# Moving weight sums, partial results and raw-weight tiles in a two-layer hybrid kernel

## The chip, the cores and the metric

The kernel runs on one core of one Trainium2 chip. TensorE (PE) multiplies matrices, VectorE (DVE) and ScalarE (ACT) do elementwise work, GpSimd (POOL) a few small operations and the transfers that add, and SyncE (SP) issues nearly all other transfers. Each engine works through its own queue in order and waits at its head. The metric is the device time of one execution in microseconds, as a median over runs.

## What is computed

Two layers on 512 tokens of width 1024, each with a mixing part and a gated feed-forward; all of it is float32.

```python
for layer in range(DEPTH):
    a = rmsnorm(h, ln_mix_pre[layer])
    mem_n = rmsnorm(mem, ln_mem[layer])
    if layer < N_A_LAYERS:
        ...
        main = chunked_spatial_gating(u, v, w_spatial[layer], b_spatial[layer],
                                      ln_v_g[layer], ln_v_b[layer])
    else:
        ...
        main = forgetting_attention(q, k_s, v_s, log_f_s)
    mixed = jnp.concatenate([main, memory_attention(q_mem, mem_n, w_mem_kv[layer])], axis=-1)
    h = h + rmsnorm(mixed @ w_out[layer], ln_mix_post[layer])
    f = rmsnorm(h, ln_ffn_pre[layer])
    f = (jax.nn.silu(f @ w_ffn_gate[layer]) * (f @ w_ffn_up[layer])) @ w_ffn_down[layer]
    h = h + rmsnorm(f, ln_ffn_post[layer])
```

The feed-forward is 2816 wide (22 blocks of 128). The change touches it most.

## The kernel before

**Numbers in two parts.** Every float32 operand is cut by `split` (L266) into a high part, which ScalarE rounds, and a low part, which VectorE subtracts; `mm3` (L208) multiplies by three matmuls (high by high, high by low, low by high). So each block of weights costs one ScalarE cast `whi` and one VectorE subtraction `wlo` before PE can use it.

**Feed-forward with seven products.** `feed_forward` (L1171) runs blocks 0 and 1 in the ordinary way at the boundary before it. The other 20 blocks are taken in pairs, m = 2, 4, ... 20, and each pair of gate weights and of up weights is one `Seven` (L1028): the 2 by 2 blocks of weights a11, a12, a21, a22 are multiplied by seven products in place of eight, in the order 1, 7, (3 of the set before), 6, 4, 2, 5. A product is 12 matmuls of 256 columns. Product 7 needs the sum s3 = a11 + a21, and a21 + a22 goes into the place of a21 (L1055, L1056); products 6 and 3 need a further addition each (L1059, L1061). Product 4 adds to the bank of product 7, after ScalarE has copied that out (L1083).

**Sums made by DMA.** For the gate weights of m = 6 to 20, and for the down weights, `sums_ahead` (L162) makes the two sums in DRAM: SP issues a copy from DRAM to DRAM (a gate sum is one of 512 KB), and POOL an accumulating transfer on top of it, which waits for the copy. `to_sum` is the list of those still to make; each call makes one, queued in SP behind the last load of weights. Before the change `sets` (L1249) calls it ahead of each gate set and each up set, so that 16 sums a layer are made while the gate and up sets run. For such a gate set the sums are loaded in place of one block, and the quarter a22 apart (L1041). The up weights are summed by VectorE.

**Down pass.** After each pair m = 2 + 2j up to j = 7, `Down` (L1102) holds u0, u1 and t, and `straight` (L1255) adds product 2 of the block before into two PSUM banks `kept`. Then a first pass over the eight blocks takes products 0, 3, 6, 5, a second takes 1 and 4 (`first_pass` L1309, loop L1332); `tap` (L1289) adds the ends to `ys`, the sums of the down projection, in which the products of blocks 0 and 1 already stand. Blocks 18 and 20 follow as gate and up sets without a Down; they and their four down blocks end in the tail.

**Space.** Raw weights go through four tiles of 4 KB per partition (`raw_tile` L134): two per set, so that a load waits until the set but one before it is done with its tiles. `act` is a ring of 36 tiles of 2 KB, `plain` one of 12. The residual stream `h` (16 KB per partition) is written to DRAM as `kept_h` (L1201) while the feed-forward runs; its space, `room` (L1222), holds u1 of the eight blocks (L1228) and is given back before sets 18 and 20, when h is loaded again (L1361).

**Order.** The program's order gives priorities. A planner takes them and its own costs and fixes the order on each engine's queue (SP's and POOL's among them) before the kernel runs; an instruction whose inputs it sees ready earlier can be drawn forward. `behind` (L253) pins the instructions made inside it behind a given one on the same engine.

**POOL's other work.** The reciprocal roots of the norms run there (`rsqrt` L280): one per 128 tokens in the tails, two in each boundary (L312), one in layer A for the layer norm. `boundary` (L938) joins a tail, the norm and the first four blocks of the next stage.

Of the kernel before, what the change touches and what calls it, by code (L numbers as in the profile page):

```python
# [1 line left out]

# [40 lines left out]
def hybrid(ctx: ExitStack, tc: tile.TileContext, i: dict, out: bass.AP):  # L43
# [93 lines left out]
    def loaded(src):  # L137

        raw = raw_tile()
        last_load[0] = nc.sync.dma_start(raw, src)  # L140
        return raw

    def prepared(src, shape, eng=None):
# [4 lines left out]
        last_load[0] = nc.sync.dma_start(dst, src)  # L148
# [11 lines left out]
    two_sums, to_sum = {}, []  # L160
# [22 lines left out]
    def moving_pair(src, aside=False):  # L183

        raw = wp.tile([P, 1024], F32, tag="raw", name=name("raw"), bufs=4)
        last_load[0] = nc.sync.dma_start(raw.rearrange("p (m c) -> p m c", m=4), src)
# [401 lines left out]
    def layer_a():  # L588
# [83 lines left out]
        with tc.tile_pool(name="sgu", bufs=1) as lp:  # L672
# [148 lines left out]

            gate_inputs(0)
# [205 lines left out]
    class Seven:  # L1028
# [5 lines left out]
        def __init__(self, xs, w, layer, m, tag, rows, room=None):  # L1034
            self.xs, self.tag, self.rows, self.room = xs, tag, rows, room
            self.parts = {}
            if (w, layer, m) in two_sums:
                both, raw = loaded(two_sums[w, layer, m]), loaded(i[w][layer, m])
# [4 lines left out]
            else:  # L1043
                raw, more = loaded(i[w][layer, m]), loaded(i[w][layer, m + 1])
# [4 lines left out]
        def form(self, n):  # L1049

            a11, a12, a21, a22 = self.a11, self.a12, self.a21, self.a22
            if n == 7:
                if not self.summed:
                    self.s3 = temp("s3")
                    V.tensor_add(self.s3, a11, a21)  # L1055
                    V.tensor_add(a21, a21, a22)  # L1056
                return self.s3
# [44 lines left out]
    class Down:  # L1102
# [33 lines left out]
        def weights(self, which):  # L1136

            four = lambda t: t.rearrange("p (m c) -> p m c", m=4)
# [4 lines left out]
            elif which == 1:  # L1143
                raw, t = four(raw_tile()), four(temp("t"))
# [4 lines left out]
            else:  # L1149
                raw = raw_tile()  # L1150
# [20 lines left out]
    def feed_forward(layer, phase, xp, meanwhile=None):  # L1171
# [28 lines left out]
        close()  # L1200
        kept_h = dp.tile([P, KT, T], F32, tag=name("rows"), name=name("rows"))  # L1201
# [10 lines left out]
        ys = [[None] * 2 for _ in range(TB)]  # L1212
        kept = [ps("tr", s="x") for _ in range(2)]
        for tb, dh in [(t, d) for d in (1, 0) for t in range(2)] + [(t, d) for t in (2, 3) for d in range(2)]:
# [3 lines left out]
            if tb > 1 or dh:  # L1218
                ys[tb][dh] = plain("y")
                A.activation(ys[tb][dh], o, AF.Copy, scale=1.0 - 2 * dh)  # L1220
# [66 lines left out]
        one, two = [act("ua", F32) for _ in range(2)], [act("ub", F32) for _ in range(2)]  # L1287

        def tap(n):  # L1289

            for t in range(2):
                x, y = o[n][t], ys[t]
                z = ys[2 + t]
                if n == 0:
                    A.copy(one[t], x)
                    V.tensor_add(y[0], x, y[0])
                elif n == 3:
                    V.tensor_add(one[t], x, one[t])
                elif n == 6:
                    V.tensor_add(two[t], x, one[t])  # L1300
                elif n == 5:
                    V.tensor_add(z[0], x, z[0])
# [6 lines left out]
        def first_pass(j, some):  # L1309
            if 0 in some:  # L1310
                downs[j].weights(1)
# [10 lines left out]
        for t in range(2):  # L1322
            ys[t][0] = plain("y")
            A.copy(ys[t][0], kept[t])
# [6 lines left out]
        late = [(z, t, d) for z, d, some in ((2, 0, two), (2, 1, two), (0, 1, one)) for t in range(2)]  # L1331
        for j, d in enumerate(downs):  # L1332
            d.weights(2)
# [4 lines left out]
            if j < len(late):  # L1338
                z, t, dh = late[j]
# [351 lines left out]
```

## Time and profile before

| | us |
|---|---|
| median of 3 runs | 1109.92 |
| lowest and highest | 1109.91, 1111.99 |
| the profiled execution | 1112.7 |
| its span, first to last instruction | 1111.0 |
| granted TensorE clock | 0.998 of full |

In the span, layer A with its boundary runs to about 200 us, the first feed-forward to about 503, layer B from there to about 790, and the second feed-forward with its tail to the end. In rows of the profile, `out<-in` names the tiles written and read, buffer numbers left out; `x` counts instructions; what stands after the last bar, or in square brackets, is the idle time of the engine just before, and what ended it. A tile has the name that it was given first where space is shared, so `room` stands for u1 of a Down, and `s`, `u` for rows of a set.

### The profile page before, as it was taken

Reading aid. Unit: us, or ns where it says so; the run is one execution under the profiler, and the core shown is the slowest. Engines: PE = TensorE matmul, PEld = TensorE weight load, DVE = VectorE, ACT = ScalarE, POOL = GpSimd, SP = SyncE. Lnnn points to the kernel's source line nnn. Section 1 sums busy time; section 2 is a strip of 40 time slices with the busy share of each in tenths; the row PEclk is TensorE's granted clock in tenths of the full one; section 3 lists DMA queues with packets and bytes.
Section 4 is the critical chain, followed back from the end, with each engine's and each line's share of the span. In section 5 each row is a group of like instructions: output and inputs, shape, how many; then the busy total and the mean of one; then the engine's idle time right before and its main releaser. Section 6 shows DMA issues by size and latency. Waiting matters only on the chain.

```text
span 1111.0 us, 19990 instructions
## 1 busy us (share of the span) xinstructions
PE 1086.8 (98%) x7286; PEld 984.2 (89%) x7286; DVE 936.6 (84%) x1839; ACT 729.6 (66%) x1609; POOL 59.6 (5%) x74
## 2 busy tenths in 40 slices
PE   9999999999999899999999999999999999899997
PEld 7998889999999888998988898889999999888996
DVE  7889658998877999996987798858898887999975
ACT  7776468666565667676765677768665665666563
POOL 0100001001100000000000000011011010000000
PEclk9999999999999999999999999999999999999999
DMA  7422346499888545653222654545489888544622
GB/s 267 157 81 76 96 114 199 115 239 220 217 204 203 144 130 152 218 171 127 84 92 75 173 127 108 148 114 171 125 220 235 219 210 217 143 124 135 215 77 76
DMA packets 126379, 172.69 MB, mean 155 GB/s; under 512 B 7821, under 2 KB 91801, under 8 KB 126281
## 3 DMA queue, kind: packets, MB, share of 16 engines
q1 hardware_dynamic: 114920, 153.93, 45.3%
q0 software_dynamic: 10944, 17.30, 10.3%
q8 instruction: 57, 0.93, 0.3%
q14 instruction: 42, 0.34, 0.1%
q10 hardware_dynamic: 416, 0.18, 0.1%
HBM read 155.04 MB, written 39.85 MB: 175 GB/s over the span
## 4 chain that ended last, share of the span: by engine, by line
PE 71%; DVE 12%; DMA 6%; ACT 6%; issue 4%; POOL 0%; SPq 0%; DVEq 0%; POOLq 0%; ACTq 0%
DVE wlo L268 5%; PE y L210 4%; PE y L211 4%; PE y L212 4%; DMA raw<-in_w_up 3%; PE a L210 3%; PE a L211 3%; PE a L212 3%; PE ps L212 3%; PE ps L211 3%; PE ps L210 3%; PE p L210 3%; PE p L212 3%; PE p L211 3%; ACT whi L267 2%
## 5 line engine op out<-in xcount | busy, mean ns | idle before, releaser
L267 ACT CAST whi<-raw 128x512 fp32r<-128x512 f32 x476 | 285.8, 619 | 93.9 <-DMA raw<-in_w_gate 24.4
L268 DVE TENSOR_TENSOR wlo<-raw,whi 128x512 fp32r<-128x512 f32 x476 | 318.3, 684 | 28.8 <-ACT whi L267 23.0
L210 PE MATMUL a<-xshi,whi 128*128 128x256 f32 x480 | 135.4, 282 | 2.0 <-ACT e L1094 2.0
L211 PE MATMUL a<-xslo,whi 128*128 128x256 f32 x480 | 134.7, 281 | 0.0
L212 PE MATMUL a<-xshi,wlo 128*128 128x256 f32 x480 | 134.5, 280 | 0.0
L210 PEld LDWEIGHTS a<-xshi,whi 128*128 128x128 f32 x480 | 90.3, 188 | 4.1 <-ACT e L1094 3.3
L211 PEld LDWEIGHTS a<-xslo,whi 128*128 128x128 f32 x480 | 90.4, 188 | 0.7
L212 PEld LDWEIGHTS a<-xshi,wlo 128*128 128x128 f32 x480 | 90.4, 188 | 0.0
L210 PE MATMUL e<-t,whi 128*128 128x256 f32 x160 | 47.2, 295 | 11.1 <-ACT s L1083 5.7
L211 PE MATMUL ps<-xslo,whi 128*128 128x256 f32 x192 | 53.9, 283 | 0.6 <-DVE xslo L268 0.6
L212 PE MATMUL ps<-xshi,wlo 128*128 128x256 f32 x192 | 54.3, 285 | 0.0
L210 PE MATMUL ps<-xshi,whi 128*128 128x256 f32 x192 | 53.6, 287 | 0.0
L210 PE MATMUL y<-whi,mixedhi 128*128 128x512 f32 x128 | 51.6, 403 | 0.0
L211 PE MATMUL y<-wlo,mixedhi 128*128 128x512 f32 x128 | 50.6, 395 | 0.0
L210 PE MATMUL p<-whi,ff 128*128 128x512 f32 x128 | 50.6, 396 | 0.0
L212 PE MATMUL y<-whi,mixedlo 128*128 128x512 f32 x128 | 50.4, 394 | 0.0
L211 PE MATMUL p<-wlo,ff 128*128 128x512 f32 x128 | 50.4, 394 | 0.0
L212 PE MATMUL p<-whi,ff 128*128 128x512 f32 x128 | 50.2, 394 | 0.0
L869 DVE TENSOR_TENSOR y<-y,y 128x512 f32<-128x512 f32 (+1 forms) x33 | 22.2, 673 | 30.4 <-PE y L212 30.3
L210 PE MATMUL e<-t3hi,whi 128*128 128x256 f32 x160 | 45.0, 281 | 0.0
L211 PE MATMUL e<-t,whi 128*128 128x256 f32 x160 | 45.0, 281 | 0.0
L210 PE MATMUL x<-xshi,whi 128*128 128x256 f32 x160 | 44.9, 281 | 0.0
(356 smaller groups left out, 3492.6 us busy)
## 6 DMA issues: line engine op xcount, KB each, us to landing
raw<-in_w_up SPq DMA_DIRECT2D x44, 512.0 KB, 4.5
raw<-in_w_gate SPq DMA_DIRECT2D x28, 512.0 KB, 4.6
raw<-in_w_down SPq DMA_DIRECT2D x28, 512.0 KB, 3.7
raw<-in_w_out SPq DMA_DIRECT2D x16, 512.0 KB, 4.5
sums<-in_w_gate SPq DMA_DIRECT2D x16, 512.0 KB, 6.0
sums<-in_w_gate POOLq DMA_DIRECT2D x16, 512.0 KB, 5.7
sums<-in_w_down SPq DMA_DIRECT2D x32, 256.0 KB, 4.8
sums<-in_w_down POOLq DMA_DIRECT2D x16, 512.0 KB, 6.9
```

The source lines that it names most:

```text
L210: PE.matmul(o, w[0], x[0], start=start, stop=False, skip_group_check=more)
L211: PE.matmul(o, w[0], x[1], start=False, stop=False, skip_group_check=more)
L212: return PE.matmul(o, w[1], x[0], start=False, stop=stop, skip_group_check=more)
L267: last_hi[0] = A.copy(hi, src)
L268: last_split[0] = last_hi[0], (eng or V).tensor_sub(lo, src, hi)
L869: (V.tensor_sub if turned_sign and dh else V.tensor_add)(y, o[:, cols], y)
```

## The change

It has four parts that share space.

1. `more_raws`: the space `room` becomes four raw tiles, handed out in turn. The up sets from m = 4 on (18 and 20 among them), the gate set m = 4, and every second block in both down passes take theirs there. So `room` is in use until the last up set, and h is loaded after that. u1 moves to the `plain` ring.
2. `kept_y`: the six results of the down products of blocks 0 and 1 that were kept in `plain` go to DRAM and are read back in the second pass, at j = 1 to 6. Four results of the taps now live in `act`, and the copies of `kept` in the two tiles tagged `acc`. The products of half 0 come first.
3. The eight gate sums of a layer are put on the list in layer A (for the first feed-forward) and in layer B (for the second). `load`, through which the loads of weights now go, counts 0.5 or 0.8 of a sum for each load and makes one whenever a whole one is due. In the feed-forward `sets` makes one down sum per pair, and none before the up set.
4. The two VectorE additions for an unsummed set are pinned behind the last split that was traced before them.

```diff
-    def loaded(src):
-        raw = raw_tile()
-        last_load[0] = nc.sync.dma_start(raw, src)
+    def loaded(src, raw=None):
+        raw = raw_tile() if raw is None else raw
+        load(raw, src)
         return raw
...
-    two_sums, to_sum = {}, []
+    two_sums, to_sum, credit = {}, [], [0, 0]
+
+    def load(dst, src):
+
+        last_load[0] = nc.sync.dma_start(dst, src)
+        credit[1] += credit[0]
+        if credit[1] >= 1:
+            credit[1] -= 1
+            sums_ahead()
...
+            to_sum.extend(("w_gate", 0, 6 + 2 * j) for j in range(8))
+            credit[0] = 0.5
             gate_inputs(0)
...
-                    V.tensor_add(self.s3, a11, a21)
-                    V.tensor_add(a21, a21, a22)
+                    with behind(last_split[0][1]):
+                        V.tensor_add(self.s3, a11, a21)
+                        V.tensor_add(a21, a21, a22)
...
-        for j in range(2, ones):
-            to_sum.append(("w_gate", layer, 2 + 2 * j))
-            if j > 2:
-                to_sum.append(("w_down", layer, 2 * j - 4))
-        to_sum.extend(("w_gate", layer, m) for m in (18, 20))
-        to_sum.extend(("w_down", layer, m) for m in (12, 14, 16))
+        to_sum.extend(("w_down", layer, 2 + 2 * j) for j in range(ones))
...
-        for tb, dh in [(t, d) for d in (1, 0) for t in range(2)] + [(t, d) for t in (2, 3) for d in range(2)]:
+        for tb, dh in [(t, d) for d in range(2) for t in range(2)] + [(t, d) for t in (2, 3) for d in range(2)]:
...
-                ys[tb][dh] = plain("y")
-                A.activation(ys[tb][dh], o, AF.Copy, scale=1.0 - 2 * dh)
+                y = plain("y")
+                A.activation(y, o, AF.Copy, scale=1.0 - 2 * dh)
+                nc.sync.dma_start(kept_y[tb, dh], y)
...
+        places_of_raws = cycle([room[:, 2 * n : 2 * n + 2, :].rearrange("p a b -> p (a b)") for n in range(4)])
+
+        def more_raws():
+            return next(places_of_raws)
...
-            downs.append(Down(layer, 2 + 2 * j, act("u", F32), room[:, j, :],
+            downs.append(Down(layer, 2 + 2 * j, act("u", F32), plain("u"),
...
             sums_ahead()
-            yield Seven(xs, "w_gate", layer, m, "mm", gate_rows)
-            sums_ahead()
-            yield Seven(xs, "w_up", layer, m, "lg", lambda row, u: up_rows(row, u, some), None if some else places)
+            yield Seven(xs, "w_gate", layer, m, "mm", gate_rows, raws=more_raws if m == 4 else None)
+            yield Seven(xs, "w_up", layer, m, "lg", lambda row, u: up_rows(row, u, some), None if some else places,
+                        more_raws if m > 2 else None)
...
                 if n == 0:
+                    one.append(act("ua", F32))
                     A.copy(one[t], x)
-                    V.tensor_add(y[0], x, y[0])
+                    y[0] = act("ya", F32)
+                    V.tensor_add(y[0], x, aside[t])
...
                 elif n == 5:
-                    V.tensor_add(z[0], x, z[0])
+                    z[0] = act("yb", F32)
+                    V.tensor_add(z[0], x, two[t])
...
-                downs[j].weights(1)
+                downs[j].weights(1, more_raws if j % 2 else None)
...
-            ys[t][0] = plain("y")
-            A.copy(ys[t][0], kept[t])
+            aside.append(temp("aside", tag="acc", bufs=2))
+            A.copy(aside[t], kept[t])
...
-            d.weights(2)
+            d.weights(2, more_raws if j % 2 else None)
...
-            if j < len(late):
-                z, t, dh = late[j]
-                y = ys[z + t][dh]
-                V.tensor_add(y, (two if z else one)[t], y)
+            if 0 < j < 7:
+                tb, dh, some = late[j - 1]
+                y = plain("y")
+                nc.sync.dma_start(y, kept_y[tb, dh])
+                if some is None:
+                    V.tensor_add(ys[tb][dh], y, ys[tb][dh])
+                else:
+                    V.tensor_add(y, y, some)
+                    ys[tb][dh] = y
...
+        to_sum.extend(("w_gate", 1, 6 + 2 * j) for j in range(8))
+        credit[0] = 0.8
         fill = queue([query_block(m) for m in range(2, 6)] + [value_block(0), key_block(0), key_block(1), value_block(1), key_block(2), key_block(3),
                       value_block(2), key_block(4), key_block(5)])
```

`prepared` and `moving_pair` load through `load` as well. After the boundary of a feed-forward `credit[0]` is set to 0 and the rest of the list is made at once; in layer B it is set to 0 when the output projection is laid out.

More of the change, by code (lines that the diff above doesn't have):

```diff
@@ L1043, in __init__ @@
             else:
-                raw, more = loaded(i[w][layer, m]), loaded(i[w][layer, m + 1])
+                raw, more = loaded(i[w][layer, m], raws()), loaded(i[w][layer, m + 1], raws())
                 self.a21, self.a22 = more[:, :512], more[:, 512:]
@@ L1286, in feed_forward @@
         o = {0: [ps("mm", s="p") for _ in range(2)], 3: [ps("lg", s="p") for _ in range(2)]}
-        one, two = [act("ua", F32) for _ in range(2)], [act("ub", F32) for _ in range(2)]
+        one, two, aside = [], [], []
         def tap(n):
@@ L1330, in feed_forward @@
         o.update({1: [ps("mm", s="q") for _ in range(2)], 4: [ps("lg", s="q") for _ in range(2)]})
-        late = [(z, t, d) for z, d, some in ((2, 0, two), (2, 1, two), (0, 1, one)) for t in range(2)]
+        late = [(2 + t, 0, None) for t in range(2)] + [(z + t, 1, some[t]) for z, some in ((2, two), (0, one))
+                                                       for t in range(2)]
         for j, d in enumerate(downs):
-            d.weights(2)
+            d.weights(2, more_raws if j % 2 else None)
             for n in (1, 4):
```

23 lines of the change are left out of this document (16 added, 7 removed).

## The prediction

> **What bounds the kernel now.** I read the page first: its busy line and its row of DMA tenths.
>
> ```profile
> PE 1086.8 (98%) x7286; PEld 984.2 (89%) x7286; DVE 936.6 (84%) x1839; ACT 729.6 (66%) x1609; POOL 59.6 (5%) x74
> DMA  7422346499888545653222654545489888544622
> ```
>
> TensorE is busy for 98% of the span, so nothing is to be won except where it waits, and the DMA row has two plateaus of 8 and 9 tenths. They are the gate and up stages of the two feed-forwards. The second view is the busy time by stage, with these two stages, what follows each, and stretches for comparison.
>
> ```profile
> 210.00:372.00 162.00, 156.81 (x1272) 153.23 (x1272) 136.86 (x240) 98.98 (x223) 13.92 (x13) 1.00 0.81 209
> 372.00:400.00 28.00, 26.00 (x141) 21.76 (x140) 27.15 (x52) 18.34 (x41) 0.00 (x0) 1.00 0.53 150
> 400.00:420.00 20.00, 20.00 (x88) 16.16 (x87) 19.21 (x37) 13.70 (x30) 0.00 (x0) 1.00 0.42 117
> 460.00:500.00 40.00, 40.00 (x336) 39.67 (x335) 37.42 (x66) 29.21 (x63) 1.14 (x2) 1.00 0.51 151
> 800.00:955.00 155.00, 151.08 (x1229) 147.80 (x1229) 131.80 (x230) 95.45 (x215) 14.01 (x13) 1.00 0.84 218
> 955.00:980.00 25.00, 23.03 (x136) 19.65 (x135) 24.15 (x47) 15.26 (x36) 0.00 (x0) 1.00 0.50 137
> 1040.00:1060.00 20.00, 20.00 (x171) 20.00 (x171) 18.98 (x32) 14.29 (x31) 0.00 (x0) 1.00 0.48 147
> ```
>
> Columns: the stretch, its length, busy time and instructions of PE, PEld, DVE, ACT and POOL, the granted clock, the DMA share, GB/s. The clock is full everywhere. The stretch 460 to 500 runs the same code on blocks 18 and 20 (gate sums ready in DRAM, no straight products and no new sums). There PE takes 40.00/336 = 0.119 us for a 256-column matmul, with DVE at 37.42 of 40. The stages of 162 and 155 us are slower per matmul at a DMA share of 0.81 and 0.84. Next I looked for what PE waits for in them: the groups of PE by line (205 to 400, then 795 to 985), and the list of waits (the same two stretches).
>
> ```profile
> L210 PE MATMUL e<-t,whi 128*128 128x256 f32 x64 | 19.1, 299 | 6.2 <-ACT s L1083 3.6 <-ACT room L1083 2.3
> L210 PE MATMUL e<-t,whi 128*128 128x256 f32 x64 | 19.0, 297 | 4.9 <-ACT room L1083 2.8 <-ACT s L1083 2.1
> ```
>
> ```profile
> ACT ff L267 <- DVE room L1239: 14.1, 6, 2.7
> DVE s L1055 <- DMA raw<-in_w_up: 13.9, 5, 3.2
> ...
> DVE s L1055 <- DMA raw<-in_w_up: 11.9, 6, 3.4
> ```
>
> Nearly all of PE's idle time is at one place, product 4 of a set, which cannot begin before ScalarE has copied product 7 out of the same bank (L1083). The timeline of one such case shows why that copy is late.
>
> ```profile
> 347.21 5.01 SPq L140 DMA_DIRECT2D raw<-in_w_up  x2
> ...
> 357.87 0.69 DVE L1055 TENSOR_TENSOR s<-raw,raw 128x512 f32<-128x512 f32 x1 [3.23 <-DMA raw<-in_w_up]
> ...
> 361.49 0.68 DVE L1239 SCALAR_TENSOR_TENSOR room<-room,s 128x512 f32<-128x512 f32 x1
> ...
> 362.26 0.41 ACT L267 CAST ff<-room 128x256 fp32r<-128x256 f32 x1 [2.71 <-DVE room L1239]
> 362.57 0.61 ACT L267 CAST whi<-raw 128x512 fp32r<-128x512 f32 x1
> 363.09 0.37 ACT L1083 COPY s<-e 128x256 f32<-128x256 f32 x1
> ...
> 363.51 0.19 PEld L210 LDWEIGHTS e<-t,whi 128*128 128x128 f32 x1 [1.47 <-ACT s L1083]
> ```
>
> The second load of the up block goes out at 347.21 + 5.01 - 0.33 = 351.9, since its tile is free only then; it lands near 357.8. VectorE has the sum s at the head of its queue and stands for 3.23 us with splits behind it. So room (L1239) is late, ScalarE waits 2.71 for it with the copy two places behind, and PE stands. One late load moves through DVE, ACT and PE.
>
> **The change part by part.** *Raw tiles and sums moved.* The up sets from m = 4 on, and the gate set m = 4, take their two tiles from the space of h, so that loads of either kind are two sets ahead instead of one. The eight gate sums of a layer, each one copy and one accumulate of 512 KB, leave the stage.
>
> ```profile
> raw<-in_w_up SPq DMA_DIRECT2D x44, 512.0 KB, 4.5
> ...
> sums<-in_w_gate SPq DMA_DIRECT2D x16, 512.0 KB, 6.0
> sums<-in_w_gate POOLq DMA_DIRECT2D x16, 512.0 KB, 5.7
> ...
> h<-rows SPq DMA_DIRECT2D x8, 512.0 KB, 9.9
> ```
>
> A set of seven products is 84 matmuls, 10 us, so a load that now starts two sets (20 us) ahead of its use has 14 us to spare over the 5.9 us that the bad one took. The up load's wait at DVE, 13.9 and 11.9 us, should go whole. What that is worth is PE's time: the matmuls of a stage at the rate of 460 to 500. The stage holds straight products, six matmuls of 512 columns each; by the groups of PE by shape there are three rows like this one, 36 in all, in either stage:
>
> ```profile
> L211 PE MATMUL x<-wlo,ff 128*128 128x512 f32 x12 | 4.7, 393 | 0.0
> ```
>
> They cost 20.00/88 = 0.227 us each by the row of 400 to 420. First layer: (1272 - 36) x 0.119 + 36 x 0.227 = 155.3, so 162.0 - 155.3 = 6.7 us. Second: 1193 x 0.119 + 8.2 = 150.2, so 155.0 - 150.2 = 4.8. Together **11.5**. Bounds: at the best rate seen, 20.00/171 = 0.117 from 1040 to 1060, it is 9.2 + 7.2 = 16.4; if no more than the half of the waits goes, 5.7. DVE is not in the way as long as it stays below PE: 136.86 us of work in the 155.3 us left is 88%, less than the 94% of the stretch I measure by.
>
> The Trainium skill (Perfetto Trace Analysis, Identifying the Most-Contended Engine) says that the busy share of matmuls is a poor measure of how near TensorE is to its limit, and that of weight loads a better one. By it the two stages, at 94.6% and 95.4% of weight loads against 99.2% in 460 to 500, would give 7.5 + 6.0 = 13.5 us, near the sum above; the page's 89% over the whole span would promise ten times that, and there the trace disagrees with the rule: 400 to 420 has 16.16 of 20 at PE's full pace, because a 512-column matmul hides its load.
>
> *The transition to the down pass*, 372 to 400 and 955 to 980: PE idles 2.0 us in each, with DVE at 27.15 of 28. The change gives DVE no less work, so I take 0; DVE might come in with less backlog, so at best 4.0.
>
> *Sums pinned.* The two additions of an up set are queued behind the split of that set's product 1, which reads the same tile. Without the pin, loads that come early would draw them further forward. No instruction is added; 0, with the waits above already counted.
>
> *First down products in DRAM.* Six tiles of 256 KB per layer are written behind ScalarE's copies and read back in the second pass, 12 transfers a layer. ScalarE's copies are the same six, DVE's additions the same count (the late ones run at j = 1 to 6 instead of 0 to 5, two taps take another operand). The writes stand in SP's queue for the copies; the loads behind them are those of m = 4, which so far went out 7 us after the last copy's end:
>
> ```profile
> 204.32 0.60 ACT L1220 ACTIVATE y<-y 128x512 f32<-128x512 f32 x1 [0.79 <-PE y L212]
> ...
> 212.20 0.94 SPq L140 DMA_DIRECT2D raw<-in_w_gate  x2
> ```
>
> DMA is at 0.42 in the down pass. I take 0; a read that is late stops DVE's addition and the splits behind it, at most one landing, 4.5 us by the row of the up loads, per layer.
>
> *h comes back later.* Its space is in use to the last up set. The last split of raw weights of the second feed-forward and the first residual addition:
>
> ```profile
> 1070.95 0.69 DVE L268 TENSOR_TENSOR wlo<-raw,whi 128x512 fp32r<-128x512 f32 x1 [0.16 <-ACT whi L267]
> ...
> 1088.84 0.86 DVE L907 SCALAR_TENSOR_TENSOR h<-yt,gains,h 128x128 f32<-128x128 f32 x3
> ```
>
> 17.2 us lie between, and the reload's landing took 9.9; 7 us to spare, cost 0. Were the cover gone, each us late would lengthen the end by one.
>
> *Four results now sit in the ring of 36* that also holds the memory inputs of the next layer.
>
> ```profile
> L272 ACT ACTIVATE mparts<-mem,gains x8: 493/502/511, 441.6 to 452.3; 128x256 fp32r<-128x256 f32 x8
> ...
> L210 PE MATMUL ps<-mparts,whi x16: 277/280/283, 490.4 to 497.3; 128*128 128x256 f32 x16
> ```
>
> They are made 38 us ahead of their use. With four places fewer, half of them or the first ff tiles wait for the last set to give up its inputs; eight casts of 0.5 us then fall at its end. 0, at worst 2.
>
> *Sums in layers A and B.* Sixteen copies in SP's queue behind loads, sixteen accumulates in POOL's. Stretches of those layers have room, and PE never waits there:
>
> ```profile
> 40.00:140.00 100.00, 99.92 (x606) 88.32 (x606) 82.75 (x185) 66.04 (x142) 1.64 (x2) 1.00 0.29 90
> 500.00:600.00 100.00, 100.00 (x640) 90.02 (x639) 82.09 (x188) 67.93 (x155) 7.10 (x12) 1.00 0.30 93
> ```
>
> But POOL also does the reciprocal roots on which the boundaries hang, in order, and an accumulate waits there for its copy. Before, this mixture was already there:
>
> ```profile
> 150.62 1.04 POOL L181 DMA_DIRECT2D sums<-in_w_gate  x1 [0.92 <-DMA sums<-in_w_gate]
> 154.61 0.57 POOL L281 TENSOR_TENSOR r<-v,mhalf 128x1 f32<-128x1 f32 x1 [2.95 <-DVE v L876]
> ...
> 183.53 0.88 POOL L181 DMA_DIRECT2D sums<-in_w_gate  x1 [1.21 <-DMA sums<-in_w_gate]
> 187.46 1.09 POOL L281 TENSOR_TENSOR r<-var,mhalf 128x2 f32<-128x2 f32 x1 [3.05 <-DVE var L311]
> ```
>
> Both times POOL was free again 3 us before the root's input came. I take **1.0** for one accumulate that stands in front of a root on the path; from 0 to 6.0 + 0.9 = 6.9 for each one that waits a whole landing.
>
> Sum: 11.5 - 1.0 = 10.5 us. The profiled execution ran 1112.7 (its span 1111.0 and 1.7 around it) and would come to 1102.2; the runs' median, 1109.92, lies 2.8 below it, so I expect **1099.4**.
>
> **The rivals.** *All stalls of both feed-forwards go*: best rate and no idle transitions, 16.4 + 4.0 = 20.4, 1089.5. For it: nothing but these stages stalls. Against: DVE at 27.15 of 28 in the transition.
>
> *Half only.* DVE and ACT keep an order in which product 4 waits for L1083 even when loads are early, or SP's queue is held by another transfer (the quarter a22 and the straight block share four small tiles), so loads don't start two sets ahead. For it: both layers idle 2.0 us in the transition, where no load is waited for. Against: the largest waits hang on the load. Half of 11.5 less 1.0: 1105.2. If the loads went out no earlier at all, the change would not do what it says: about 1110, within 0.2%.
>
> *Slower: POOL's queue.* Sums made near a boundary put accumulates in front of its roots, each waiting for a copy that stands behind a load in SP's queue. Price 6.9 us each on the path; it decides from the second one on (2 x 6.9 > 11.5), and with three, 20.7 - 11.5 = 9.2 us slower, 1119.1. For it: the tail's and boundary's own loads carry sums. Against: SP runs ahead there, so that the copies are done before most roots (the boundary's first gate load goes out 24 us before the root of 154.61), and the two cases above cost nothing.
>
> ```profile
> 130.82 0.34 SPq L148 DMA_DIRECT2D raw<-in_w_gate  x1
> ```
>  The Trainium skill (SBUF — State Buffer, the box on the "DVE blocks DMA" trap) adds that a DMA issued from POOL may stand while VectorE holds a port they share. The landings of 5.7 from POOL and 6.0 from SP for the same 512 KB, in stages where DVE is busy 85% of the time, show none of it.
>
> **How the numbers follow.** Forecast 0.60, all stalls gone 0.08, half only 0.13, no effect 0.04, slower 0.15. Faster by over 0.2% (2.2 us, about what a measurement of this kernel can tell from no change) is 0.60 + 0.08 + 0.13 = 0.81, less 0.02 for half cases eaten by the other costs: 0.79; same 0.04; slower 0.17. The forecast's own range is 1093.5 (16.4 gained) to 1105. The range reaches from 1091, short of the first rival, to 1112, which takes in the half and no effect and leaves out most of the slower case, some 0.18 in all.
>
> **What would show it.** Right: the waits of L1055 for raw<-in_w_up are gone, PE's idle time at product 4 falls from 6.2 and 4.9 us to below 2, the DMA share of the stages falls from 0.81 towards 0.5, and the stages are 6.7 and 4.8 us shorter. Layers A and B keep their length. Wrong: idle time at L1083 without a load behind it (half only), POOL's waits for sums ahead of L281 and ACT's for r L281 grown (slower), or DVE waiting for the reads of kept_y or h.

## The result and the profile after

The changed kernel took 1095.44 us, median of 4 runs (1094.50 to 1095.71), where the kernel before, measured beside it, took 1110.95 (4 runs, 1109.91 to 1112.79). The ratio is 0.9857, 95% interval 0.9840 to 0.9874: 15.5 us less. Measured a second time it took 1094.68 (1094.34 to 1095.10), ratio 0.9835 (0.9811 to 0.9860). The profiled execution, 1094.5 with a span of 1092.8, is 18.2 us shorter than the profiled one of before; the medians differ by less, because the profiled run of before lay 1.8 above its median and that of after 0.9 below.

The row of DMA tenths on the page of after:

```profile
DMA  7554875867644447267592654535877553546232
```

The plateaus of 8 and 9 in the feed-forwards are gone. Busy time of after by the stretches of the prediction (columns as there):

```profile
210.00:372.00 162.00, 161.99 (x1329) 159.81 (x1328) 148.59 (x252) 109.44 (x237) 6.22 (x5) 1.00 0.61 169
372.00:400.00 28.00, 28.00 (x123) 22.52 (x122) 27.43 (x55) 19.27 (x43) 0.00 (x0) 1.00 0.50 139
800.00:955.00 155.00, 155.00 (x1251) 151.87 (x1251) 142.71 (x248) 104.79 (x228) 6.25 (x5) 1.00 0.60 167
955.00:980.00 25.00, 25.00 (x109) 19.98 (x108) 24.43 (x48) 17.02 (x38) 0.00 (x0) 1.00 0.50 138
```

PE lacks 0.01 us in these 370, the transitions among them, where it had lacked 2.0 in each. The groups of PE by line, product 4 in 205 to 400 and in 795 to 985:

```profile
L219 PE MATMUL e<-t,whi 128*128 128x256 f32 x64 | 18.0, 281 | 0.0
...
L219 PE MATMUL e<-t,whi 128*128 128x256 f32 x58 | 16.3, 281 | 0.0
```

Idle time ahead of product 4 went from 6.2 and 4.9 to 0.0. VectorE's list of waits holds no wait for an up load any more.

To see where the 18.2 us are, four events serve as marks: the last copy of a first down product (ScalarE), the first root of layer B (GpSimd), that copy in the second feed-forward, and the first root of the tail. From the timeline of before (its first mark, 204.32, stands in the prediction):

```profile
511.32 0.57 POOL L281 TENSOR_TENSOR r<-v,mhalf 128x1 f32<-128x1 f32 x1 [9.85 <-DVE v L876]
...
790.89 0.60 ACT L1220 ACTIVATE y<-y 128x512 f32<-128x512 f32 x1 [0.79 <-PE y L212]
...
1085.66 0.57 POOL L281 TENSOR_TENSOR r<-v,mhalf 128x1 f32<-128x1 f32 x1 [150.34 <-DVE v L876]
```

and of after:

```profile
203.48 0.60 ACT L1233 ACTIVATE y<-y 128x512 f32<-128x512 f32 x1 [0.79 <-PE y L221]
...
500.01 0.57 POOL L290 TENSOR_TENSOR r<-v,mhalf 128x1 f32<-128x1 f32 x1 [9.39 <-DVE v L887]
...
781.45 0.60 ACT L1233 ACTIVATE y<-y 128x512 f32<-128x512 f32 x1 [0.79 <-PE y L221]
...
1067.91 0.57 POOL L290 TENSOR_TENSOR r<-v,mhalf 128x1 f32<-128x1 f32 x1 [185.97 <-DVE v L887]
```

The differences of neighbouring marks: first feed-forward 307.00 before, 296.53 after (10.47 less); layer B 279.57 and 281.44 (1.87 more); second feed-forward 294.77 and 286.46 (8.31 less). With 0.84 ahead of the first mark and 0.45 behind the last that makes the 18.2. So the feed-forwards gave 18.8 and layer B took 1.9 back. In the second measurement layer B took 280.34, 0.8 more than before, so that part of the loss differs from one execution to the next.

### The profile page after: what moved, and what is told of

Its sections match the earlier page's. It is cut to its first block, busy times and chain, and to the rows that moved or that the text cites. A ratio compares the mean times of both kernels' runs of the same rounds, so it can differ in the third digit from the quotient of the medians.

```text
span 1092.8 us, 20047 instructions
## 1 busy us (share of the span) xinstructions
PE 1080.9 (99%) x7286; PEld 982.6 (90%) x7286; DVE 941.6 (86%) x1839; ACT 736.9 (67%) x1609; POOL 59.4 (5%) x74
## 4 chain that ended last, share of the span: by engine, by line
PE 89%; ACT 3%; DMA 3%; DVE 2%; issue 1%; POOL 1%; SPq 0%; POOLq 0%; DVEq 0%; ACTq 0%
PE a L219 7%; PE a L221 7%; PE a L220 7%; PE e L219 3%; PE e L220 3%; PE e L221 3%; PE ps L221 3%; PE ps L220 3%; PE ps L219 3%; PE y L219 3%; PE y L220 3%; PE y L221 3%; PE p L219 3%; PE p L221 3%; PE p L220 3%; PE x L219 3%
## 5 line engine op out<-in xcount | busy, mean ns | idle before, releaser
L277 DVE TENSOR_TENSOR wlo<-raw,whi 128x512 fp32r<-128x512 f32 x316 | 210.8, 685 | 21.4 <-ACT whi L276 18.2
L276 ACT CAST whi<-raw 128x512 fp32r<-128x512 f32 x316 | 189.0, 619 | 56.2 <-PE a L220 14.6
L276 ACT CAST whi<-room 128x512 fp32r<-128x512 f32 x160 | 98.3, 621 | 47.9 <-PE x L220 9.5
L277 DVE TENSOR_TENSOR wlo<-room,whi 128x512 fp32r<-128x512 f32 x160 | 108.7, 686 | 6.4 <-ACT whi L276 3.8
L276 ACT CAST ff<-u 128x256 fp32r<-128x256 f32 x80 | 32.3, 406 | 29.3 <-PE p L221 15.4
L220 PE MATMUL x<-xslo,whi 128*128 128x256 f32 x160 | 44.9, 281 | 0.0
```

Source lines behind the costliest of these rows:

```text
L220: PE.matmul(o, w[0], x[1], start=False, stop=False, skip_group_check=more)
L276: last_hi[0] = A.copy(hi, src)
L277: last_split[0] = last_hi[0], (eng or V).tensor_sub(lo, src, hi)
```

## The experiments

Twelve runs. The columns F1, B and F2 are the three stretches above, in us, each from that run's one profiled execution. Where a feed-forward is the same as in after, F1 or F2 agrees with it within 0.06 us; B is less steady. Each ratio is to before measured beside the run; there the medians of before were 1111.29 (7 runs; the first four rows below after), 1112.43 (17; b_sums_moved_copies, a_again, a_sums_after_boundary, a_sums_in_boundary) and 1112.40 (23; the rest). One of the four executions of a_sums_in_ffn took 1106.08, which pulls its ratio up, and one of the ten of a_sums_in_boundary 2726, which nothing here explains.

| run | what it is | median us | ratio, 95% interval | F1 | B | F2 |
|---|---|---|---|---|---|---|
| (before) | | 1110.95 | | 307.00 | 279.57 | 294.77 |
| (after) | | 1095.44 | 0.9857 (0.9840 to 0.9874) | 296.53 | 281.44 | 286.46 |
| b_sums_moved | before + sums moved | 1098.01 | 0.9874 (0.9855 to 0.9893) | 297.36 | 280.48 | 288.23 |
| a_no_extra_raws | after, four raw tiles | 1097.60 | 0.9876 (0.9858 to 0.9894) | 297.54 | 282.35 | 287.19 |
| a_sums_in_ffn | after, sums as before | 1096.70 | 0.9895 (0.9847 to 0.9943) | 298.22 | 279.90 | 288.39 |
| a_no_pin | after, no pin | 1096.61 | 0.9867 (0.9847 to 0.9886) | 297.37 | 280.13 | 286.97 |
| b_sums_moved_copies | b_sums_moved + copies nothing reads | 1097.89 | 0.9862 (0.9835 to 0.9888) | 298.88 | 280.29 | 288.67 |
| b_pin | before + pin | 1097.82 | 0.9868 (0.9844 to 0.9893) | 298.61 | 279.91 | 289.05 |
| b_sums_moved_up_slot | b_sums_moved, sums ahead of the up set | 1109.96 | 0.9982 (0.9967 to 0.9996) | 303.51 | 280.54 | 294.88 |
| b_both_at_gate | before, both sums ahead of the gate set | 1112.86 | 0.9990 (0.9972 to 1.0008) | 309.12 | 280.43 | 293.11 |
| a_again | after | 1094.68 | 0.9835 (0.9811 to 0.9860) | 296.55 | 280.34 | 286.45 |
| a_sums_after_boundary | layer B's sums behind close() | 1095.08 | 0.9848 (0.9822 to 0.9874) | 296.58 | 286.50 | 286.45 |
| a_sums_in_boundary | layer B's sums in its boundary | 1108.73 | 0.9963 (0.9946 to 0.9980) | 305.37 | 285.53 | 286.46 |
| a_behind_roots | accumulates behind roots | 1101.97 | 0.9904 (0.9882 to 0.9926) | 296.59 | 288.74 | 286.44 |

### Which part carries the gain

**b_sums_moved**: before with the sums made as in the change (gate sums in layers A and B, down sums one for each pair of sets); four raw tiles, no pin.

```diff
-        for j in range(2, ones):
-            to_sum.append(("w_gate", layer, 2 + 2 * j))
...
+        to_sum.extend(("w_down", layer, 2 + 2 * j) for j in range(ones))
...
             yield Seven(xs, "w_gate", layer, m, "mm", gate_rows)
-            sums_ahead()
             yield Seven(xs, "w_up", layer, m, "lg", lambda row, u: up_rows(row, u, some), None if some else places)
```

> The kernel before, with only the gate sums moved into layers A and B; raw tiles, results in DRAM and order of the additions as before. Late loads (my theory: a load is late because it starts one set ahead AND lands slowly): the up load still starts when its tile is free, but lands in 4 to 4.5 us instead of 5.9, so that VectorE's wait for raw<-in_w_up falls from 13.9 and 11.9 us (two feed-forwards) to 4 to 7 each and PE's idle time at product 4 from 6.2 and 4.9 us to about 3 each: 1103 to 1106 us. Traffic alone (rival): the whole gain, 1095 to 1098 us, waits near 0. Buffers alone (rival): no gain, 1109 to 1111 us, waits above 11 us in each.

Measured 1098.01: my forecast missed, and this part alone gives nearly the whole gain. The waits for up loads did not go; they got shorter. The row of the waits of b_sums_moved (waiting line, releaser, sum, times, longest):

```profile
DVE s L1065 <- DMA raw<-in_w_up: 10.9, 10, 1.5
```

Those of before were up to 3.4, 25.9 us in 11. PE lacks 0.60 us in 205 to 400 here, where it lacked 7.19 before: the short waits hardly reach it, the long ones did.

**a_no_extra_raws**: after with the ring of four raw tiles everywhere.

```diff
-            return next(places_of_raws)
+            return raw_tile()
```

> The changed kernel with all raw weights in the four old tiles again; the space of h stands empty, everything else as changed. Late loads: as with the sums moved alone, 1102 to 1106 us, VectorE's waits for the up loads 3 to 7 us in each feed-forward. Traffic alone: 1095 to 1097 us. Buffers alone: 1109 to 1111 us.

1097.60, missed too. The tiles in the space of h are not needed for most of the gain.

**a_sums_in_ffn**: after with the sums asked for where they were before.

```diff
-            to_sum.extend(("w_gate", 0, 6 + 2 * j) for j in range(8))
-            credit[0] = 0.5
...
             yield Seven(xs, "w_gate", layer, m, "mm", gate_rows, raws=more_raws if m == 4 else None)
+            sums_ahead()
             yield Seven(xs, "w_up", layer, m, "lg", lambda row, u: up_rows(row, u, some), None if some else places,
                         more_raws if m > 2 else None)
```

> The changed kernel with the gate sums made in the feed-forwards again, two sums per pair; the extra raw tiles stay. Late loads: a load that starts two sets ahead has more than 10 us to spare even at a DMA share of 0.85, so 1095 to 1099 us with PE idle under 1.5 us at product 4 in each feed-forward. Traffic alone: 1107 us or more, with waits for up loads of over 8 us. Sums come too late for their sets (a third way): VectorE or ScalarE waits for raw<-sums, 1100 us or more.

1096.70, as forecast. The busy time of 210 to 372 of this run:

```profile
210.00:372.00 162.00, 160.63 (x1317) 158.25 (x1315) 147.21 (x250) 108.47 (x236) 13.01 (x12) 1.00 0.81 214
```

The DMA share is that of before, 0.81, but PE lacks 1.37 us of the 162 and not 5.19. A high share by itself costs little; in b_pin below PE lacks 0.70 at a share of 0.83.

**a_no_pin**: after with the two additions left free.

```diff
-                    with behind(last_split[0][1]):
-                        V.tensor_add(self.s3, a11, a21)
-                        V.tensor_add(a21, a21, a22)
+                    V.tensor_add(self.s3, a11, a21)
+                    V.tensor_add(a21, a21, a22)
```

> The changed kernel without the pin of the two additions of an up set. Late loads: the pin is worth little once loads are early, 1095 to 1098 us; additions are drawn forward but their data are there. The pin carries the gain (rival): VectorE stands again for 8 us or more in a feed-forward with additions at the head of its queue, 1101 us or more.

1096.61, as forecast. Without the pin the additions are drawn forward and wait again; the row of the waits:

```profile
DVE s L1067 <- DMA room<-in_w_up: 14.3, 10, 2.4
```

but PE hardly notices: it lacks 0.41 us in 205 to 400 and 795 to 985 together, and F1 and F2 are within 0.9 us of after. So the length of VectorE's waits alone does not tell what they cost.

Each of the three can be taken out at a price of 1.2 to 2.2 us against the 1095.44 of after. These medians were taken at different times and the intervals of the ratios overlap; F1 and F2 together show 1.4 to 3.6 us. What the three have in common was still open.

### Bytes, place, or order

**b_sums_moved_copies**: b_sums_moved with the bytes given back: two copies of 512 KB from DRAM to DRAM, which nothing reads, ahead of each gate set up to m = 16.

```diff
             sums_ahead()
+            if m < 18:
+                for x in range(2):
+                    waste = dp.tile([P, 1040], F32, tag=name("waste"), name=name("waste"))[:, :1024]
+                    with behind(last_load[0]):
+                        nc.sync.dma_start(waste, i["w_gate"][layer, m + x])
```

> The kernel before with the gate sums moved into layers A and B, and in the feed-forwards, for each pair up to m = 16, two copies of 512 KB from DRAM to unused DRAM in SP's queue, about the bytes of the sum that left, without an accumulate. Traffic makes the loads late (my theory now): up loads land in 5 us or more again, VectorE waits 9 us or more for them in each feed-forward, PE idles 3 us or more at product 4 in each, 1103 to 1110 us. POOL's accumulates or their order made them late (rival): stays at 1097 to 1099 us.

1097.89: missed too. The copies stand behind the up loads of a pair and cost nothing in the median (F1 is 1.5 and F2 0.4 longer than in b_sums_moved). Bytes as such are not it. What is left is the place of a sum in the queue.

**b_sums_moved_up_slot**: b_sums_moved with its one sum per pair of sets asked for between the gate set and the up set.

```diff
-            sums_ahead()
             yield Seven(xs, "w_gate", layer, m, "mm", gate_rows)
+            sums_ahead()
             yield Seven(xs, "w_up", layer, m, "lg", lambda row, u: up_rows(row, u, some), None if some else places)
```

> The run b_sums_moved with the one sum that is left for each pair of sets asked for between the gate set and the up set, not ahead of the gate set. Theory (an accumulate that runs against the second up load makes it late): the second up loads land after 5 us or more, VectorE's waits for raw<-in_w_up go back to 2 to 3 us, time 1102 to 1110. Rival (the number and bytes of the sums matter, not where they fall): 1097 to 1099, as b_sums_moved with 1098.0.

1109.96, as the theory had it: nearly all the gain is gone, with half the sums of before in the feed-forwards. VectorE's waits are back:

```profile
DVE s L1065 <- DMA raw<-in_w_up: 26.2, 12, 3.4
```

Three timelines show how, at the same place of the first feed-forward. Before:

```profile
256.83 5.01 SPq L140 DMA_DIRECT2D raw<-in_w_up  x2
...
259.21 0.84 POOL L181 DMA_DIRECT2D sums<-in_w_gate  x1 [8.47 <-DMA sums<-in_w_gate]
...
267.06 0.69 DVE L1055 TENSOR_TENSOR s<-raw,raw 128x512 f32<-128x512 f32 x1 [2.81 <-DMA raw<-in_w_up]
...
270.68 0.68 DVE L1239 SCALAR_TENSOR_TENSOR room<-room,s 128x512 f32<-128x512 f32 x1
```

b_sums_moved:

```profile
256.43 5.01 SPq L164 DMA_DIRECT2D raw<-in_w_up  x2
...
264.93 0.69 DVE L1065 TENSOR_TENSOR s<-raw,raw 128x512 f32<-128x512 f32 x1 [1.07 <-DMA raw<-in_w_up]
```

b_sums_moved_up_slot, with the accumulate of the sum:

```profile
255.15 5.01 SPq L164 DMA_DIRECT2D raw<-in_w_up  x2
...
256.41 1.25 POOL L185 DMA_DIRECT2D sums<-in_w_down  x1 [17.59 <-DMA sums<-in_w_down]
...
264.75 0.69 DVE L1065 TENSOR_TENSOR s<-raw,raw 128x512 f32<-128x512 f32 x1 [2.18 <-DMA raw<-in_w_up]
```

The second of the two loads goes out at the start of the row + 5.01 - 0.33, so at 261.51, 261.11 and 259.83. VectorE begins to wait 2.74, 2.75 and 2.74 us later in the three (267.06 - 2.81 - 261.51, and so on), and goes on 5.55, 3.82 and 4.92 after the issue, a time that is called the landing here. So in all three the addition reaches the head of VectorE's queue 2.75 us after its load went out, and the wait is the landing less 2.75: 2.81, 1.07, 2.18. In the first and the third an accumulate went out 2.3 and 3.4 us ahead of the load; the landing is 1.7 and 1.1 us longer with it. At this one place PE hardly stands (0.28 us at 272.70 in before); what the longer landings cost together, the times of the two runs show.

**b_both_at_gate**: before with both sums of a pair ahead of the gate set.

```diff
             sums_ahead()
+            sums_ahead()
             yield Seven(xs, "w_gate", layer, m, "mm", gate_rows)
-            sums_ahead()
             yield Seven(xs, "w_up", layer, m, "lg", lambda row, u: up_rows(row, u, some), None if some else places)
```

> The kernel before with both sums of a pair of sets asked for ahead of the gate set, none between gate and up; count and bytes as before. Theory (the accumulate against the second up load is what hurts): the up loads come about 1.5 to 2 us earlier and most of the gain is there, 1097 to 1103. Rival (count and bytes of the accumulates in the feed-forwards matter): 1108 to 1111.

1112.86: missed. Half of the theory held, the other half not. The waits of this run:

```profile
ACT whi L267 <- DMA raw<-in_w_gate: 34.1, 15, 5.2
...
DVE s L1055 <- DMA raw<-in_w_up: 10.2, 11, 1.2
```

and of before:

```profile
ACT whi L267 <- DMA raw<-in_w_gate: 24.4, 17, 2.5
```

The waits for up loads are as short as in b_sums_moved, 1.2 at most (the median landing of all 44 is 4.5 as in before, against 3.6 there). But now the gate loads have the two accumulates beside them. The case of the longest wait:

```profile
252.10 0.33 SPq L140 DMA_DIRECT2D raw<-in_w_gate  x1
253.11 0.85 POOL L181 DMA_DIRECT2D sums<-in_w_gate  x1 [1.97 <-DMA sums<-in_w_gate]
...
261.58 0.62 ACT L267 CAST whi<-raw 128x512 fp32r<-128x512 f32 x1 [5.19 <-DMA raw<-in_w_gate]
```

The other accumulate went out at 249.87. The load takes 9.5 us to its cast, ScalarE stands 5.19 of them with the copies out of PSUM behind it, and PE waits 2.72 for such a copy at 262.53. A sum hurts the load that it runs beside, here a gate load, above an up load.

**b_pin**: before with the pin and nothing else.

```diff
-                    V.tensor_add(self.s3, a11, a21)
-                    V.tensor_add(a21, a21, a22)
+                    with behind(last_split[0][1]):
+                        V.tensor_add(self.s3, a11, a21)
+                        V.tensor_add(a21, a21, a22)
```

> The kernel before with the pin alone (the two additions of a set without stored sums tied behind the split of product 1). Theory (the up loads stay late, as an accumulate still runs against each second up load): 1107 to 1111, the waits for raw<-in_w_up stay at 2 to 3 us. Rival (the pin carries a large part of the gain by itself): 1100 or less.

1097.82: the rival was right. Of b_pin, the median landing of the up loads on its page, the one wait that is left, and the same place of the timeline:

```profile
raw<-in_w_up SPq DMA_DIRECT2D x44, 512.0 KB, 5.0
```

```profile
DVE s L1056 <- DMA raw<-in_w_up: 0.9, 1, 0.9
```

```profile
256.51 5.01 SPq L140 DMA_DIRECT2D raw<-in_w_up  x2
...
266.50 0.69 DVE L1240 SCALAR_TENSOR_TENSOR room<-room,s 128x512 f32<-128x512 f32 x1
...
268.06 0.68 DVE L1056 TENSOR_TENSOR s<-raw,raw 128x512 f32<-128x512 f32 x1
```

The loads are as slow as ever, a median of 5.0 us against 4.5. But the addition stands 6.87 us behind the issue of its load (268.06 - 261.19) instead of 2.75, and the work on room, which the chain needs, is done ahead of it at 266.50, where it came at 270.68 before. Eleven waits of 25.9 us together are one of 0.9. ScalarE's waits for gate loads fall as well, from 24.4 to 12.5; what share of the gain goes with them the run does not separate. An edit that moves two instructions in a queue wins 14.1 (8.39 + 5.72) of the 18.8 us in F1 and F2, and 14.6 us of the time (1112.40 to 1097.82).

### Sums ahead of roots in layer B

In after, an accumulate in POOL's queue stands ahead of roots. Its timeline:

```profile
506.31 0.90 POOL L190 DMA_DIRECT2D sums<-in_w_gate  x1 [5.74 <-DMA sums<-in_w_gate]
506.96 0.85 POOL L290 TENSOR_TENSOR r<-v,mhalf 128x1 f32<-128x1 f32 x1
507.85 0.72 ACT L906 ACTIVATE ya<-ya,r 128x512 f32<-128x512 f32 x1 [3.12 <-POOL r L290]
...
520.58 0.39 PE L221 MATMUL ps<-xshi,wlo 128*128 128x256 f32 x1 [0.96 <-DVE wlo L277]
```

The root follows the accumulate at once and ScalarE waited 3.12 for it. At 520.58 PE stands 0.96 us. That the one leads to the other is not shown: in a_again ScalarE waits 3.09 at the same place, and PE lacks only 0.04 us from 500 to 540.

**a_again** (after as it is) and **a_sums_after_boundary** (layer B's sums put on the list only behind the boundary):

```diff
         close()
+        to_sum.extend(("w_gate", 1, 6 + 2 * j) for j in range(8))
+        credit[0] = 1
...
-        to_sum.extend(("w_gate", 1, 6 + 2 * j) for j in range(8))
-        credit[0] = 0.8
```

> The changed kernel once more, as the measure for the next runs: 1095 to 1096 us on every theory.

> The changed kernel with the gate sums of the second feed-forward put on the list only after layer B's boundary is closed, one per load. POOL's queue costs something there (my theory after the profile: an accumulate waited 5.7 us ahead of a root, ScalarE 3.1 us for that root, and PE 1.0 us later on): ScalarE's waits for r L290 fall back to about 9 us in all, the PE wait for wlo near 520 us is gone, 1094 to 1095 us, 0.5 to 1.5 below the changed kernel. POOL costs nothing (rival): same time as the changed kernel within 0.3 us, the PE wait stays.

1094.68 and 1095.08, no difference shown, so the theory of 0.5 to 1.5 us is not borne out. The profiled execution of the second was the longest of its six, 1101.79, and shows what the hazard can cost. Its timeline:

```profile
533.79 0.91 POOL L190 DMA_DIRECT2D sums<-in_w_gate  x1 [12.85 <-DMA sums<-in_w_gate]
537.60 0.82 POOL L190 DMA_DIRECT2D sums<-in_w_gate  x1 [2.91 <-DMA sums<-in_w_gate]
538.18 1.00 POOL L290 TENSOR_TENSOR r<-var,mhalf 128x2 f32<-128x2 f32 x1
...
539.23 0.57 PE L287 MATMUL rb<-ident,r 128*128 128x128 f32 x2 [4.88 <-POOL r L290]
```

Two accumulates stand ahead of the boundary's root, though the sums were asked for behind the boundary in the program. VectorE had the root's input ready at 532.75, and PE waits 4.88 us for the root.

**a_sums_in_boundary**: all eight of layer B's sums tied to the loads of the tail and the boundary, the prediction's slower rival as a run.

```diff
+        to_sum.extend(("w_gate", 1, 6 + 2 * j) for j in range(8))
+        credit[0] = 1
         a, close = boundary(phase, G_FFN_POST, G_MIX_PRE + 1, bnorm, rbc,
...
-        to_sum.extend(("w_gate", 1, 6 + 2 * j) for j in range(8))
-        credit[0] = 0.8
```

> The changed kernel with all eight gate sums of the second feed-forward tied to the eight loads of layer B's tail and boundary, the suspected cost put up on purpose. POOL's queue costs: accumulates wait for their copies ahead of two or more of the six roots between 495 and 545 us, PE idles 3 to 8 us there, 1098 to 1104 us. It costs nothing (rival): 1095 to 1096.5 us, PE idle in the boundary as in the changed kernel.

1108.73, above the 1098 to 1104 of the forecast and 14 us more than a_again, which was measured beside it. Two waits make most of it. From its timeline, a load and then GpSimd's queue:

```profile
502.43 1.14 ACT L276 CAST whi<-raw 128x512 fp32r<-128x512 f32 x2 [7.09 <-DMA raw<-in_w_down]
...
522.14 0.86 POOL L190 DMA_DIRECT2D sums<-in_w_gate  x1 [7.26 <-DMA sums<-in_w_gate]
524.74 0.81 POOL L190 DMA_DIRECT2D sums<-in_w_gate  x1 [1.74 <-DMA sums<-in_w_gate]
525.29 0.86 POOL L290 TENSOR_TENSOR r<-v,mhalf 128x1 f32<-128x1 f32 x1
526.18 0.72 ACT L906 ACTIVATE yb<-yb,r 128x512 f32<-128x512 f32 x1 [5.76 <-POOL r L290]
```

The root behind two accumulates costs ScalarE 5.76, as the prediction's rival had it. The 7.09 at a block of the tail's weights looks like the effect of b_both_at_gate, a load with sums beside it. PE waits 5.59 us at 503.10 and 4.39 at 530.40, shortly behind the two, and the granted clock reads 0.83 in 500 to 520 and in 520 to 540.

**a_behind_roots**: after with every accumulate tied behind the last root listed ahead of it.

```diff
     def rsqrt(dst, src, n):
-        G.tensor_tensor(out=dst, in0=src, in1=mhalf[:, :n], op=ALU.pow)
+        last_root[0] = G.tensor_tensor(out=dst, in0=src, in1=mhalf[:, :n], op=ALU.pow)
...
+    def add(dst, src):
+        with behind(*filter(None, last_root)):
+            G.dma_start(dst, src, accum_op=ALU.add)
```

> The changed kernel with each accumulate of a sum tied behind the last square root listed ahead of it on GpSimd, so that none stands ahead of a boundary's root in layers A and B. Theory (accumulates ahead of roots cost layer B about 1 us, and are the cause of its single longer executions): 1093.5 to 1094.7, the stall at 520 us gone. Rival (the stall comes from the weights' traffic): 1094.5 to 1096.0, as the changed kernel.

1101.97, 6.5 and 7.3 us above the two medians of after: missed. The stall at 520 is gone as expected, which says little, as a_again has none either; but three accumulates now go out together behind the last root. Its timeline:

```profile
538.00 2.60 POOL L173 DMA_DIRECT2D sums<-in_w_gate  x3
...
553.13 0.21 ACT L280 CAST whi<-wf 128x24 fp32r<-128x24 f32 x1 [7.65 <-DMA wf<-in_w_f]
...
554.50 0.77 PE L223 MATMUL qk<-xshi,whi 128*128 128x512 f32 x1 [6.47 <-DVE q L1413]
```

and its chain of waits:

```profile
539.15 13.96 DMA wf<-in_w_f
```

A load of 48 KB went out beside them and took 13.96 us; ScalarE stood 7.65 at its cast, VectorE behind ScalarE, and PE 6.47. No version tried beat the changed kernel by more than the runs can tell.

## Why the prediction was right, and where its steps were not

**The bound and the chain.** A late up load, the addition at the head of VectorE's queue, room, ScalarE's copy, PE: b_pin breaks this chain at the addition alone and wins 14.6 us, which shows it. The time came 4.0 us under the forecast of 1099.4. Most marks named beforehand came as written: the waits gone, product 4 at 0.0, the DMA share from 0.81 to 0.61. The last of them turned out to be no sign of the cause, as b_pin wins nearly as much at 0.83. Layer B did not keep its length.

**Which part cures it** is the step that failed: "No instruction is added; 0, with the waits above already counted" for the pin, and the whole 11.5 for tiles and moved sums. Two of the three edits take most of the wait's cost away each by itself: the pin moves the waiting instruction (b_pin), the moved sums shorten the landing (b_sums_moved). The tiles, which were to start the load earlier and stood first in the prediction, were never run alone; a_sums_in_ffn has them with the pin and a_no_pin with the moved sums, so what they would do by themselves is not shown. The gains don't add up, since the edits remove the same wait: from the pin alone to all three, F1 goes from 298.61 to 296.53 and F2 from 289.05 to 286.46. That the time came near the forecast does not bear out this step, since either of the two edits alone brings it there; in this the forecast had luck.

The Trainium skill (Perfetto Trace Analysis, Optimization Strategy) says that the same gap over and over on the engine that should be full can mean that buffers are too few for the next tile. Here b_pin wins 14.6 us with no buffer added, and no run shows what more buffers alone would do; the trace asks first what else stands behind the waiting instruction.

**The size.** Of the 18.8 us won in the feed-forwards the prediction had 11.5, and two terms were too small. The first is the rate. In 210 to 360 of after PE is never idle, and the straight products there are again 36:

```profile
210.00:360.00 150.00, 150.00 (x1236) 148.43 (x1235) 137.01 (x232) 101.10 (x220) 6.22 (x5) 1.00 0.62 171
```

So a 256-column matmul takes (150.00 - 36 x 0.227)/1200 = 0.1182 us, not the 0.119 of 460 to 500. By it the work of the first stage, 1272 - 36 = 1236 such matmuls and 8.2 us of straight products, takes 1236 x 0.1182 + 8.2 = 154.3, 7.7 less than 162.0; that of the second takes 1193 x 0.1182 + 8.2 = 149.2, 5.8 less than 155.0. Together that is 13.5. A stretch of before had been taken for full pace because PE's busy time read 40.00 of 40; in its timeline matmuls start 0.15 to 0.28 us after the one ahead of them at three places, which busy time does not show. The second term is the transitions, taken at 0 with 4.0 as bound: their idle time is gone whole, as PE lacks 0.01 us in 205 to 400 and none in 795 to 985. 13.5 + 4.0 = 17.5; the last 1.3 of 18.8 this sum does not place. That is the first rival's mechanism, all stalls gone, given 0.08; its 20.4 used the best rate seen anywhere, 0.117.

**The cost of sums in layers A and B**, 1.0: for layer A none shows (the first mark stands at 203.48 and 204.40 in two executions, at 204.32 before). Layer B took 1.9 more in one execution and 0.8 in the other; profiles without such sums in it read 279.57 (before), 279.90, 279.91 and 280.43, so up to 0.9 of this need not be theirs. Accumulates do stand ahead of roots, as at 506.31, but what makes up the loss stays open: in the first execution PE waits 0.96 us at 520.58 and 1.08 at 607.27 for another load (0.40 for the same one before), in a_again 0.82 for that load and nothing near 520. Where an accumulate held up a root on the path, PE or ScalarE waited 4.88 and 5.76, below the 6.9 taken for a whole landing. The slower rival's place was right, its point of decision not reached as the sums are spread.

**The rest.** Products kept in DRAM, the later reload of h and the ring of 36, each taken at 0: neither VectorE's nor ScalarE's list of waits names a read of the kept products or of h, and the end from the tail's first root is 24.89 us against 25.34.

## What to carry to other kernels

When an engine that works in order waits for a load, look at the distance in its queue between the waiting instruction and the instruction that sets the load free, and at what stands behind it: moving the waiter alone was worth as much here as moving the sums alone (1097.82 and 1098.01), and cost no memory. Cures of one wait don't add up, so try each alone before giving memory for it. Ask of every background transfer which load it runs beside, not how many bytes it moves: by its place a sum cost next to nothing, made a load land 1 to 2 us later, or came with a stall of 5 to 7 us on ScalarE.

## What was not expected of the hardware

**The clock can halve after a short wait.** In b_both_at_gate, PE waits 1.77 us ahead of 308.40. Its busy time by single microseconds from there (the granted clock is the third figure from the end):

```profile
308.40:309.40 1.00, 1.00 (x8) 1.00 (x9) 0.97 (x2) 1.00 (x3) 0.00 (x0) 1.00 0.00 0
309.40:310.40 1.00, 1.00 (x9) 1.00 (x9) 0.91 (x3) 1.00 (x5) 0.00 (x0) 0.76 0.00 0
310.40:311.40 1.00, 1.00 (x6) 1.00 (x6) 1.00 (x2) 0.59 (x2) 0.00 (x0) 0.50 0.00 0
311.40:312.40 1.00, 1.00 (x7) 1.00 (x6) 0.73 (x2) 0.84 (x2) 0.00 (x0) 0.50 0.72 74
```

About 1.5 us after the wait the clock falls to 0.50, and it stays there for 3.4 us, to 313.3. PE reads as fully busy all the while, but in the timeline its matmuls start 0.213 us apart there and not 0.118, so it loses 3.4 - 3.4 x 0.118/0.213 = 1.5 us on top of the wait. Of the four longest waits of PE in the feed-forwards of this run, 2.58, 2.72, 1.77 and 2.14 us, the last three came with such a fall, 3.4 us long each time; with 2.72 and 2.14 it began at about the end of the wait. In the 6.47 of a_behind_roots the clock fell too (0.66 in 550 to 560); with the waits of before, 1.4 us at most in the feed-forwards, it did not. The Trainium skill (TensorE: Matmul & The Clock Gate, What's actually happening) puts the fall to half clock after an idle window of about 3.4 us. Here a wait of 1.77 us was followed by a fall and one of 2.58 was not, so a wait shorter than that can be enough, and its length alone does not decide; what else does was not tried.

**A small load can be the slowest.** In a_behind_roots the 48 KB of wf took 13.96 us beside sums and weights, where the accumulates of 512 KB from 530 to 560 landed in 8.5 (median of 5).
